# A two-block transformer kernel on one core: 80 steps of the experts' hidden layer in two-part float32r, and hi and lo runs of weights in pairs

## The chip, the cores and the metric

The kernel runs on one core of one Trainium2 chip. The metric is device time in microseconds, from the start of one execution to its end. TensorE (PE) multiplies, VectorE (DVE), ScalarE (ACT) and GpSimd (POOL) do the elementwise work, and SyncE (SP) issues most of the DMA transfers. Weights come from HBM once each; nothing is kept from one execution to the next.

## The reference

One input of 256 tokens by 2048 features goes through two blocks, all in float32. The first block is a mixer (a causal pooling half and a gated linear recurrence half), a projection `w_out`, and then a product-key expert layer. Its core, cut:

```python
def chunk(zc):                       # 128 tokens
    q = (zc @ peer_wq)...            # 8 heads, two halves of 128
    ... top 16 of each half, top 16 of their sums -> expert (16 of 16384 per head), gate = softmax
    u = jnp.take(peer_u, expert, axis=0)
    act = jax.nn.gelu(jnp.einsum('chkd,cd->chk', u, zc))
    v = jnp.take(peer_v, expert, axis=0)
    w = gate * act
    return jnp.einsum('chk,chkd->cd', w, v)
```

The second block projects to queries, keys, values, gates and a gated convolution (`w_in_2`), attends, merges (`w_sb_out_2`, `w_conv_out_2`, `w_o_2`), and ends in a feed-forward part: `relu(h @ w_up)**2 @ w_down`, 2048 to 8192 and back.

## The kernel before

Features lie on the 128 partitions, tokens along the free axis: a matmul takes 128x128 weights as its stationary operand and the tokens as its moving one. The program is a list of **steps**, filled in order and then played by one loop at the end of the kernel. A step is 128 output features; it has two halves, each with a **piece** of weights of 512 KB (`[128, 8, 128]` float32), so a half is 8 matmuls (k = 0 to 7).

There are two kinds of steps. A **plain** step (`whole_step`, matmuls on line 188) multiplies the weights `wx` as they came, in plain float32. An **f32r** step (`k16` and `k8x2`) splits weights and activations: ACT copies `wx` into `wh` (type float32r, line 1354, the hi part), DVE, in one stage with POOL, writes `wl = wx - wh` (line 1365, the lo part), and the activations are held as two parts side by side, `z[:, k, 0]` and `z[:, k, 1]`. A half is then a run of 8 **hi** matmuls (line 123, `wh` times both parts, 512 columns) and a run of 8 **lo** matmuls (line 126, `wl` times the first part, 256 columns). `k16` accumulates over 2048 features, two halves into one PSUM tile; `k8x2` over 1024, each half its own.

The expert layer avoids a gather of u and v rows for most tokens: for 176 of the 256 (`ND`), all 16384 experts' hidden values are computed, 128 steps of u (`u_step`: the plain product of `peer_u` with `zn`, the normalized tokens; `post_u` applies Gelu into one of seven `hidden` buffers of 8 steps each), then multiplied by a scattered gate matrix (`make_w`, line 863, with the list `Gt` that comes from a buffer `Gd` in HBM), and 128 v steps add the products with `peer_v` into the residual `R` (`post_v`, line 904). The first 48 u steps (`LEAD`) stand alone; then u and v steps alternate, u first, and the last 48 v steps stand alone again. For the other 80 tokens (`NG`), the rows are fetched: 160 **units**, each an indirect DMA of 1 MB by POOL (line 740) into one of three buffers `ga`, and a pass of DVE over 128x2048 elements (lines 756 and 764). Units are placed along the plain pieces at an even distance.

Weights come through a **ring** of 12 tiles of 512 KB (`stream`, `RING`). `take` hands out the next tile and asks that the one 12 before has been read in program order; `wx`, `wh` and `wl` of a piece each take one. `ahead(p)` issues the transfers of coming pieces on SP: always up to piece p + 3, and in a row of plain pieces as far as the ring goes. In the loop, piece p's matmuls follow `hi(p + 3)` on ACT and stand ahead of `lo(p + 3)` on DVE. `tick` lets the waiting tasks (evacuations, `make_w`) add their instructions after each piece, `need` ticks until a named result has been put into the program. `tasks` are ticked every time, `bg` ones while a budget lasts. Each engine works through its own instructions in program order.

PSUM has four accumulators (`mm`). The base pool holds R, the two-part activations (tag A), and two buffers B0 and B1 that hold, one after the other, the mixer's outputs, the search lists, hidden values, attention outputs and feed-forward activations.

## Time and profile before

| | |
|---|---|
| median of 3 runs | 2977.0 us (2976.8 to 2977.24) |
| the profiled execution | 2975.82 us |
| its span, first to last instruction | 2974.1 us |
| PE, DVE, ACT, POOL busy | 2941.1, 1916.8, 1079.7, 348.5 us |
| first and last plain u matmul; first and last v matmul (starts) | 348.8, 1382.8; 628.8, 1623.8 us |

The profile has the span in 40 slices of 74 us; in the rows of digits each is the busy share in tenths. In groups, `x` is the number of instructions, then come the busy time in us, the mean of one in ns, and the engine's idle time ahead of them with what ended it. Matmuls overlap, so the time that one costs is the distance between starts, not its own duration. One plain float32 matmul has two records on PE, one of f32r has one.

### The profile page before, as it was taken

What the parts mean: (1) busy time and instruction counts of PE and PEld (TensorE: products, weight loads), DVE (VectorE), ACT (ScalarE), POOL (GpSimd) and SP (SyncE); (2) the same over time, 40 slices, a digit from 0 to 9 for tenths busy, and PEclk for the clock granted to TensorE, in tenths of its full rate; (3) what the DMA queues carried; (4) which work ended last, traced back from release to release, by engine and by line L of the source; (5) the groups of instructions that cost most, each with busy time, mean ns of one, the idle gap of its engine ahead of it and who ended that gap; (6) DMA issues with size and microseconds to landing.
All of it is one profiled execution on the core that took longest, in us unless ns stands there. A gap on an engine that the chain in (4) does not pass through costs nothing.

```text
span 2974.1 us, 46400 instructions
## 1 busy us (share of the span) xinstructions
PE 2941.1 (99%) x18156; PEld 2735.0 (92%) x18156; DVE 1916.8 (64%) x3260; ACT 1079.7 (36%) x1774; POOL 348.5 (12%) x321
## 2 busy tenths in 40 slices
PE   9999999999999999999999999999999999999997
PEld 7888999999999999999999888888887888888886
DVE  8877885644444444445524889886658667776777
ACT  7755325500000000000003676657555444444444
POOL 0102221112122222222102000001500000000000
PEclk9999999999999999999999999999999999999999
DMA  6465699999999999999965555555654655555553
GB/s 235 159 200 197 212 306 344 352 387 414 395 396 395 392 400 399 398 393 395 388 219 169 176 172 179 183 174 192 204 181 145 203 191 188 186 172 198 198 191 128
DMA packets 208619, 773.46 MB, mean 260 GB/s; under 512 B 21536, under 2 KB 44384, under 8 KB 187488
## 3 DMA queue, kind: packets, MB, share of 16 engines
q1 hardware_dynamic: 161136, 588.46, 56.0%
q0 software_dynamic: 23984, 169.31, 14.4%
q10 hardware_dynamic: 23280, 12.72, 1.4%
q8 instruction: 144, 2.36, 0.3%
q14 instruction: 75, 0.61, 0.1%
HBM read 755.25 MB, written 13.63 MB: 259 GB/s over the span
## 4 chain that ended last, share of the span: by engine, by line
PE 94%; DVE 2%; ACT 2%; DMA 1%; issue 1%; SPq 0%; ACTq 0%; DVEq 0%
PE mm L188 41%; PE mm L123 33%; PE mm L126 17%; PE g L800 1%; DMA Gd<-gst 1%; DVE wl L1365 1%; ACT wh L1354 0%; DMA wx<-in_w_in_dram 0%; PE s L586 0%; PE g L778 0%; DMA R<-in_x_dram 0%; DVE R L1461 0%; PE s L246 0%; DVE Y L1460 0%; DMA wx<-in_w_down_dram 0%
## 5 line engine op out<-in xcount | busy, mean ns | idle before, releaser
L1354 ACT ACTIVATE wh<-wx 128x1024 fp32r<-128x1024 f32 (+1 forms) x579 | 609.2, 1054 | 682.2 <-PE mm L123 286.0
L1365 DVE TENSOR_TENSOR wl<-wx,wh 128x1024 fp32r<-128x1024 f32 (+2 forms) x579 | 694.9, 1207 | 158.7 <-ACT wh L1354 152.7
L123 PE MATMUL mm<-z,wh 128*128 128x512 f32 x2816 | 718.0, 397 | 12.9 <-ACT wh L1354 7.0
L188 PE MATMUL mm<-zn,wx 128*128 128x176 f32 x4096 | 633.3, 313 | 0.0
L188 PEld LDWEIGHTS mm<-zn,wx 128*128 128x128 f32 x4096 | 614.5, 190 | 0.1
L123 PEld LDWEIGHTS mm<-z,wh 128*128 128x128 f32 x2816 | 510.1, 190 | 109.5 <-ACT wh L1354 7.5
L904 DVE TENSOR_TENSOR R<-R,mm 128x176 f32<-128x176 f32 x256 | 86.1, 336 | 536.4 <-PE mm L188 532.1
L126 PEld LDWEIGHTS mm<-z,wl 128*128 128x128 f32 x2816 | 384.2, 191 | 29.6 <-DVE wl L1365 2.4
L126 PE MATMUL mm<-z,wl 128*128 128x256 f32 x2816 | 393.0, 283 | 1.1 <-DVE wl L1365 0.9
L188 PE MATMUL mm<-hd,wx 128*128 128x176 f32 x2048 | 313.5, 313 | 0.0
L188 PE MATMUL mm<-hb,wx 128*128 128x176 f32 x2048 | 312.7, 313 | 0.0
L188 PEld LDWEIGHTS mm<-hd,wx 128*128 128x128 f32 x2048 | 307.5, 190 | 0.0
L188 PEld LDWEIGHTS mm<-hb,wx 128*128 128x128 f32 x2048 | 306.9, 190 | 0.0
L123 PE MATMUL mm<-f,wh 128*128 128x512 f32 x1024 | 256.7, 392 | 0.2 <-DVE f L1261 0.2
L123 PEld LDWEIGHTS mm<-f,wh 128*128 128x128 f32 x1024 | 184.2, 189 | 33.5 <-DVE f L1261 0.7
L853 ACT ACTIVATE hd<-mm 128x176 f32<-128x176 f32 x64 | 20.3, 317 | 422.1 <-PE mm L188 412.8
L853 ACT ACTIVATE hb<-mm 128x176 f32<-128x176 f32 x64 | 20.3, 317 | 402.6 <-PE mm L188 393.4
L740 POOL DMA_INDIRECT ga<-in_peer_v_rows_dram,idx x80 | 107.0, 1338 | 399.0 <-DVE ga L764 214.8
L740 POOL DMA_INDIRECT ga<-in_peer_u_rows_dram,idx x80 | 99.7, 1246 | 449.3 <-DVE hid L756 378.8
L756 DVE CUSTOM_DVE_ANT_0 ga<-ga 128x2048 f32<-128x2048 f32 x64 | 146.0, 2284 | 7.3 <-DMA ga<-in_peer_u_rows_dram,idx 7.3
L126 PEld LDWEIGHTS mm<-f,wl 128*128 128x128 f32 x1024 | 139.7, 190 | 9.9
L764 DVE SCALAR_TENSOR_TENSOR ga<-ga,hid 128x2048 f32<-128x2048 f32 x63 | 147.8, 2346 | 0.2
(373 smaller groups left out, 2528.4 us busy)
## 6 DMA issues: line engine op xcount, KB each, us to landing
wx<-in_peer_u_dram SPq DMA_DIRECT2D x256, 512.0 KB
wx<-in_peer_v_dram SPq DMA_DIRECT2D x256, 512.0 KB
wx<-in_w_in_dram SPq DMA_DIRECT2D x191, 512.0 KB
wx<-in_w_up_dram SPq DMA_DIRECT2D x128, 512.0 KB
wx<-in_w_down_dram SPq DMA_DIRECT2D x128, 512.0 KB
wx<-in_w_out_dram SPq DMA_DIRECT2D x32, 512.0 KB
wx<-in_peer_wq_dram SPq DMA_DIRECT2D x32, 512.0 KB
wx<-in_w_o_dram SPq DMA_DIRECT2D x32, 512.0 KB
```

The costliest lines, as they stand in the source:

```text
L123: pe.matmul(ps, w[0][:, k], z[:, k0 + k], start=first and k == 0, stop=False, skip_group_check=True)
L126: pe.matmul(ps[:, 0], w[1][:, k], z[:, k0 + k, 0], start=False, stop=last and k == 7, skip_group_check=True)
L188: pe.matmul(ps, w[:, k], rhs(half, k), start=k == 0 and (split or half == 0), stop=k == 7 and (split or half == 1), skip_group_check=True)
L740: pool.indirect_dma_start(out=x, out_offset=None, in_=rows, in_offset=bass.IndirectOffsetOnAxis(ap=st["idx"][i][:, s:s + 1], axis=0))
L756: dve.tensor_tensor_reduce(out=x, in0=x, in1=y, scale=1.0, scalar=0.0, op0=ALU.mult, op1=ALU.add, accum_out=h[:, s:s + 1])
L764: dve.scalar_tensor_tensor(y, x, h[:, s:s + 1], y, op0=ALU.mult, op1=ALU.add)
L800: pe.matmul(p[:, t], A[:, t], B[:, t], start=True, stop=True)
L853: act.activation(hidden(g)[:, i], ps, AF.Gelu_apprx_tanh)
L904: dve.tensor_tensor(R[:, k, NG:], R[:, k, NG:], ps, op=ALU.add)
L1354: act.activation(w[:, i:i + n], x[:, i:i + n], AF.Copy)
L1365: dve.tensor_tensor(w[:, i:i + m], x[:, i:i + m], h[:, i:i + m], op=ALU.subtract)
```

## The change

1. **u steps 48 to 127 in parts** (`part_step`): hi weights times both parts of z (352 columns), lo weights times the last `LOW` = 176 of these columns, which are the part that `parts_of_z` writes at index 1, the rounded one. `z[:, k, 1]` is the copy in float32r and `z[:, k, 0]` what is left. `post_u_part` adds the two halves of the 352 columns (ACT copy, DVE addition) and applies Gelu. The first 48 u steps and all v steps stay plain. A u step now follows the v step three places later in the list: v steps 0 to 3 stand alone, then u and v alternate.
2. **k16 steps without lag** put both hi runs ahead of both lo runs (`own["rest"]`); their `wl` tiles count as read at the end of the second half. Steps with lag (the first two or three of a stage) and `k8x2` keep their order.
3. **The ring** may look ahead over pieces in parts, which count three tiles (`n` in `ahead`); `kind` tells "whole", "part" and None apart, and the budget of `tick` is 2.1, 0.7 and 1.25.
4. **Room**: B0 and B1 become one tile B; `zr` takes the place of `zn` once the plain u steps are done with it; the second set of fetched tokens gets its transposed rows (`zt1`) only once G is built; some small tiles move to other pools.

The core of the diff:

```diff
-    def product(ps, w, z, k0, first, last):
+    def product(ps, w, z, k0, first):
         for k in range(8):
             pe.matmul(ps, w[0][:, k], z[:, k0 + k], start=first and k == 0, stop=False, skip_group_check=True)
             yield
+
+    def rest(ps, w, z, k0, last):
         for k in range(8):
             pe.matmul(ps[:, 0], w[1][:, k], z[:, k0 + k, 0], start=False, stop=last and k == 7, skip_group_check=True)
             yield
...
-            yield from product(own["ps"], w, zt, k0, half == 0, half == 1)
+            yield from product(own["ps"], w, zt, k0, half == 0)
+            if lag:
+                yield from rest(own["ps"], w, zt, k0, half == 1)
+            elif half == 0:
+                own["rest"] = rest(own["ps"], w, zt, k0, False)
+            else:
+                yield from own.pop("rest")
+                yield from rest(own["ps"], w, zt, k0, True)
...
+    def part_step(src, post, needs=((), ())):
+        own = {}
+        def lows(half, w):
+            for k in range(8):
+                z = st["zr"][:, 8 * half + k].rearrange("p a t -> p (a t)")
+                pe.matmul(own["ps"][:, 2 * ND - LOW:], w[1][:, k], z[:, 2 * ND - LOW:], start=False,
+                          stop=half == 1 and k == 7, skip_group_check=True)
+                yield
+        def mm(half, w):
+            if half == 0:
+                own["ps"] = accumulator().rearrange("p a t -> p (a t)")[:, :2 * ND]
+            for k in range(8):
+                pe.matmul(own["ps"], w[0][:, k], st["zr"][:, 8 * half + k].rearrange("p a t -> p (a t)"),
+                          start=half == 0 and k == 0, stop=False, skip_group_check=True)
+                yield
+            if half == 0:
+                own["rest"] = lows(0, w)
+            else:
+                yield from own.pop("rest")
+                yield from lows(1, w)
+                tasks.append(post(half, own["ps"]))
...
+    def parts_of_z():
+        r = rs["rs2"]
+        z = st["zr"] = st["pb"].tile([128, 16, 2, ND], F32R, name="zr", tag="zn")
+        last = None
+        for k in range(17):
+            if k < 16:
+                t = tmp.tile([128, T], F32, name="zk", tag="ev", bufs=5)[:, :ND]
+                dve.scalar_tensor_tensor(t, R[:, k, NG:], v("norm2_g", k), r[:, NG:], op0=ALU.mult, op1=ALU.mult)
+                act.activation(z[:, k, 1], t, AF.Copy)
+            if k > 0:
+                dve.tensor_tensor(z[:, k - 1, 0], last, z[:, k - 1, 1], op=ALU.subtract)
+            last = t
+            if k % 4 == 0:
+                yield
+        ready.add("zr")
...
+            h = hidden(g)[:, i]
+            yield
+            act.activation(h, ps[:, :ND], AF.Copy)
+            yield
+            dve.tensor_tensor(h, h, ps[:, ND:], op=ALU.add)
+            release("mm")
+            yield
+            act.activation(h, h, AF.Gelu_apprx_tanh)
...
+                if j == 0 and g == 0:
+                    begin.append(lambda: tasks.append(parts_of_z()))
...
-                if e < 128:
-                    u_step(e)
                 whole_step([a["peer_v"][16 * g + 2 * j], a["peer_v"][16 * g + 2 * j + 1]],
...
+                if 48 <= e - 3 < 128:
+                    part_step(src("peer_u", e - 3), post_u_part(e - 3), (["zr"], ()))
...
-            if q > p + 3 and (q > p + RING - 2 or not all(plain(i) for i in range(p, q + 1)) or not ring[-RING][1]):
+
+            n = 1 + 2 * sum(not plain(i) for i in range(p + 3, q + 1))
+            if q > p + 3 and (n > RING - 2 or not (kind(p) and kind(q)) or not all(r[1] for r in ring[-RING:][:n])):
                 return
...
-                read(q, "wx", "wh", "wl")
-        tick(2.1 if plain(p) else 1.25)
-        if "units" in st and plain(p):
+                read(q, "wh", *(["wx"] if plain(q) else []))
+
+                if not long:
+                    read(q, "wl")
+                elif half:
+                    read(q - 1, "wl")
+                    read(q, "wl")
+        tick({"whole": 2.1, "part": 0.7, None: 1.25}[kind(p)])
+        if "units" in st and kind(p):
```

PE in the first block's `w_in`, two steps, before: `mm` is the accumulator, `z1` the activations.

```order
L123 MATMUL mm_415<-z1_99,wh_322 128x512 x8
L126 MATMUL mm_415<-z1_99,wl_343 128x256 x8
L123 MATMUL mm_415<-z1_99,wh_347 128x512 x8
L126 MATMUL mm_415<-z1_99,wl_371 128x256 x8
L123 MATMUL mm_487<-z1_99,wh_376 128x512 x8
L126 MATMUL mm_487<-z1_99,wl_409 128x256 x8
```

The same place in the changed program (its lines 125 and 131):

```order
L125 MATMUL mm_414<-z1_99,wh_321 128x512 x8
L125 MATMUL mm_414<-z1_99,wh_346 128x512 x8
L131 MATMUL mm_414<-z1_99,wl_342 128x256 x8
L131 MATMUL mm_414<-z1_99,wl_362 128x256 x8
L125 MATMUL mm_486<-z1_99,wh_367 128x512 x8
L125 MATMUL mm_486<-z1_99,wh_412 128x512 x8
```

The lo run of the first half has moved behind the hi run of the second; the matmuls are the same.

PE where u and v steps alternate, before (`zn` marks u, `hb` and `hd` the hidden values of a v step):

```order
L188 MATMUL mm_6276<-zn_2527,wx_6142 128x176 x8
L188 MATMUL mm_6276<-zn_2527,wx_6157 128x176 x8
L188 MATMUL mm_6300<-hd1_3998,wx_6170 128x176 x8
L188 MATMUL mm_6312<-hd1_3998,wx_6183 128x176 x8
L188 MATMUL mm_6326<-zn_2527,wx_6196 128x176 x8
L188 MATMUL mm_6326<-zn_2527,wx_6209 128x176 x8
L188 MATMUL mm_6348<-hd1_3998,wx_6224 128x176 x8
```

And in the changed program, a pair and the first rows of the next:

```order
L201 MATMUL mm_7967<-hb_4302,wx_7861 128x176 x8
L201 MATMUL mm_7985<-hb_4302,wx_7891 128x176 x8
L225 MATMUL mm_8000<-zr_5605,wh_7935 128x352 x8
L225 MATMUL mm_8000<-zr_5605,wh_7965 128x352 x8
L217 MATMUL mm_8000<-zr_5605,wl_7961 128x176 x8
L217 MATMUL mm_8000<-zr_5605,wl_7979 128x176 x8
L201 MATMUL mm_8047<-hb_4302,wx_7981 128x176 x8
L201 MATMUL mm_8061<-hb_4302,wx_7983 128x176 x8
```

A u step's two pieces of plain weights have become four runs from four converted tiles, while v keeps its two.

DVE at the first v step, before: `hd<-hd,Gt` are the eight multiplications of the first hidden group, `ga` a fetched unit, `R<-R,mm` the first v results.

```order
L756 ISA ga,hid_3933<-ga 128x2048
L756 ISA hid_3933 128x1
L863 TENSOR_TENSOR hd_3622<-hd_3622,Gt 128x176 x2
L756 ISA ga,hid_3933<-ga 128x2048
L756 ISA hid_3933 128x1
L863 TENSOR_TENSOR hd_3622<-hd_3622,Gt 128x176 x3
L756 ISA ga,hid_3933<-ga 128x2048
L756 ISA hid_3933 128x1
L863 TENSOR_TENSOR hd_3622<-hd_3622,Gt 128x176 x3
L756 ISA ga,hid_3933<-ga 128x2048
L756 ISA hid_3933 128x1
L904 TENSOR_TENSOR R<-R,mm 128x176 x2
```

The same place in the changed program, up to the first pair of `parts_of_z` (lines 632 and 635):

```order
L944 TENSOR_TENSOR hd_3624<-hd_3624,Gt 128x176 x2
L822 ISA ga,hid_3917<-ga 128x2048
L822 ISA hid_3917 128x1
L944 TENSOR_TENSOR hd_3624<-hd_3624,Gt 128x176 x3
L632 SCALAR_TENSOR_TENSOR zk<-R,vec,ra_2604 128x176
L944 TENSOR_TENSOR hd_3624<-hd_3624,Gt 128x176
L632 SCALAR_TENSOR_TENSOR zk<-R,vec,ra_2604 128x176
L635 TENSOR_TENSOR zr<-zk,zr 128x176
```

Three more such pairs follow, then the seventh multiplication, four pairs, the eighth, and seven pairs less one; only then come two more rows of a unit and the first additions into R. The work on `zr` has come between the multiplications that the first v matmuls read.

## Rows read from the trace of the kernel before

**Rows 1.** The page: busy time, and the 40 slices' PE clock and DMA rate.

```profile
PE 2941.1 (99%) x18156; PEld 2735.0 (92%) x18156; DVE 1916.8 (64%) x3260; ACT 1079.7 (36%) x1774; POOL 348.5 (12%) x321
...
PEclk9999999999999999999999999999999999999999
...
GB/s 235 159 200 197 212 306 344 352 387 414 395 396 395 392 400 399 398 393 395 388 219 169 176 172 179 183 174 192 204 181 145 203 191 188 186 172 198 198 191 128
```

**Rows 2.** The page's groups: line, engine, operation, count, busy us, mean ns, idle before.

```profile
L1354 ACT ACTIVATE wh<-wx 128x1024 fp32r<-128x1024 f32 (+1 forms) x579 | 609.2, 1054 | 682.2 <-PE mm L123 286.0
L1365 DVE TENSOR_TENSOR wl<-wx,wh 128x1024 fp32r<-128x1024 f32 (+2 forms) x579 | 694.9, 1207 | 158.7 <-ACT wh L1354 152.7
L123 PE MATMUL mm<-z,wh 128*128 128x512 f32 x2816 | 718.0, 397 | 12.9 <-ACT wh L1354 7.0
L188 PE MATMUL mm<-zn,wx 128*128 128x176 f32 x4096 | 633.3, 313 | 0.0
...
L904 DVE TENSOR_TENSOR R<-R,mm 128x176 f32<-128x176 f32 x256 | 86.1, 336 | 536.4 <-PE mm L188 532.1
...
L188 PE MATMUL mm<-hd,wx 128*128 128x176 f32 x2048 | 313.5, 313 | 0.0
L188 PE MATMUL mm<-hb,wx 128*128 128x176 f32 x2048 | 312.7, 313 | 0.0
...
L853 ACT ACTIVATE hd<-mm 128x176 f32<-128x176 f32 x64 | 20.3, 317 | 422.1 <-PE mm L188 412.8
```

**Rows 3.** Timeline of PE at the first v step: start us, us, instructions, count.

```profile
628.76 4.94 PE L188 MATMUL mm<-hd,wx 128*128 128x176 f32 x32
633.53 4.94 PE L188 MATMUL mm<-zn,wx 128*128 128x176 f32 x32
```

**Rows 4.** Timeline of PE in the down projection.

```profile
2704.88 2.00 PE L123 MATMUL mm<-f,wh 128*128 128x512 f32 x8
2706.72 1.12 PE L126 MATMUL mm<-f,wl 128*128 128x256 f32 x8
2707.67 2.00 PE L123 MATMUL mm<-f,wh 128*128 128x512 f32 x8
```

**Rows 5.** Timelines of weight loads at 16 columns and of PE at 128.

```profile
1512.87 1.01 PEld L778 LDWEIGHTS g<-sel,zt 128*128 128x128 f32 x8
1513.80 4.78 PEld L188 LDWEIGHTS mm<-hb,wx 128*128 128x128 f32 x32
...
575.90 1.05 PE L800 MATMUL g<-hb,hb 128*128 128x128 f32 x8
576.79 2.55 PE L188 MATMUL mm<-zn,wx 128*128 128x176 f32 x16
```

**Rows 6.** The alternating stretch: busy us (count) by engine, PE clock, DMA share, GB/s.

```profile
628.80:1387.50 758.70, 758.70 (x5088) 758.70 (x5088) 348.62 (x417) 25.73 (x82) 162.79 (x120) 1.00 1.00 398
```

**Rows 7.** Waits of SP's queue, 700 to 1400 us: total, times, longest.

```profile
SPq L1330 <- PE mm L188: 569.5, 291, 2.0
```

**Rows 8.** DMA queues, 640 to 700 us: packets, MB, share.

```profile
q1 hardware_dynamic: 4031, 14.71, 61.3%
q0 software_dynamic: 1374, 10.07, 40.5%
```

**Rows 9.** Timelines of PE in a woven hi run, two windows that end at 2252.2.

```profile
2250.00 2.43 PE L123 MATMUL mm<-z,wh 128*128 128x512 f32 x10
...
2250.90 1.52 PE L123 MATMUL mm<-z,wh 128*128 128x512 f32 x6
```

**Rows 10.** Timeline of DVE ahead of the first v step; zn's durations.

```profile
619.15 0.86 DVE L863 TENSOR_TENSOR hd<-hd,Gt 128x176 f32<-128x176 f32 x2 [18.41 <-DMA Gt<-Gd]
619.93 2.28 DVE L756 CUSTOM_DVE_ANT_0 ga<-ga 128x2048 f32<-128x2048 f32 x1
...
625.52 1.25 DVE L863 TENSOR_TENSOR hd<-hd,Gt 128x176 f32<-128x176 f32 x3
...
L573 DVE SCALAR_TENSOR_TENSOR zn<-R,vec,ra x16: 387/391/1156, 261.2 to 284.0; 128x176 f32<-128x176 f32 x16
```

More of the change, by code (lines that the diff above doesn't have):

```diff
@@ L27 @@
 ND = T - NG
+LOW = ND
 EPS = 1e-6
@@ L192, in mm @@
                 tasks.append(post(half, ps))
-        steps.append((src, mm, needs, begin, 0, False, True))
+        steps.append((src, mm, needs, begin, 0, False, "whole", False))
+    def part_step(src, post, needs=((), ())):
[19 more added lines that the diff above has]
+                tasks.append(post(half, own["ps"]))
+        steps.append((src, mm, needs, None, 0, False, "part", True))
     R = base.tile([128, 16, T], F32, name="R")
@@ L698, in token_rows @@
         ga = st["ga"] = base.tile([128, 4, 2048], F32, name="ga", tag="A")
-        st["zt"] = [ga[:, 3] if i == 0 else pb.tile([128, 2048], F32, name=f"zt{i}") for i in range(len(SETS))]
+        st["zt"] = [ga[:, 3]]
         for i, (t0, n) in enumerate(SETS):
+            if i == 1:
+                yield from wait("G")
+            zg = st["zg"] if i == 0 else st["zg1"]
             for q in range(4):
@@ L842, in hidden @@
             return st[key]
[L843 removed]
+        return st["hb"][i - 3]
     def load_G(g):
@@ L1306, with kind @@
     NP = len(pieces)
+    def kind(p):
+        return steps[pieces[p][0]][6]
     def plain(p):
-        return steps[pieces[p][0]][6]
+        return kind(p) == "whole"
     ring = []
@@ L1413 @@
         s, half = pieces[p]
-        _, mm, needs, begin, lag, weave, _ = steps[s]
+        _, mm, needs, begin, lag, weave, _, long = steps[s]
         ahead(p)
```

66 lines of the change are left out of this document (39 added, 27 removed).

## The prediction

> **What bounds the kernel now.** I read the page's busy line and its slices first. TensorE is busy 2941.1 us of 2974.1, at full clock in all 40 slices: the chip is bound by the matmuls, and a change counts by what it takes off PE's queue or by the waits that it puts there [rows 1]. The slices also show the second limit: in slices 9 to 20 the DMA engines move 387 to 414 GB/s, twice what they move in the second half. Then the groups: the plain float32 steps (L188) hold 633 + 314 + 313 = 1260 us of PE, and the f32r hi and lo runs (L123, L126) most of the rest, without idle time worth naming in front of them [rows 2]. The timeline of the stage in which u and v steps alternate shows one step of each, 32 records long: 628.76 to 633.53, 4.77 us a step and 9.55 us a pair, or 149 ns a record of 176 columns; a matmul of plain float32 is two such records, 298 ns [rows 3]. The timeline of the down projection gives the price of f32r: a run of eight hi matmuls of 512 columns takes 1.84 us (2704.88 to 2706.72), 230 ns each, eight lo matmuls of 256 columns 0.95 us, 119 ns each [rows 4].
>
> **Edit 1: the u steps 48 to 127 in parts.** Each loses 16 matmuls of 298 ns (4.77 us) and gets 16 hi matmuls of 352 columns and 16 lo matmuls of 176. Neither width is in the trace.
> - Hi, 352 columns: from below, the plain record, which streams twice 176 columns in 149 ns [rows 3]; from above, the 512-column matmul of 230 ns less its 160 columns more, which at 2.4 GHz are 67 ns: 163 ns [rows 4]. The cost of the same kind of operand is the nearer one; I take 160.
> - Lo, 176 columns: from above, the 256-column matmul, 119 ns [rows 4]; from below, the same in proportion, 119 x 176/256 = 82 ns. Between them stands the weight load. In the additions of the fetched rows the moving operand has 16 columns, and still eight weight loads take 0.93 us (1512.87 to 1513.80), 116 ns each; the one-hot products of 128 columns go at 0.89/8 = 111 ns [rows 5]. So small columns do not go below some 110 ns when every matmul has new weights, and each lo matmul has. I take 114. The Trainium skill, "TensorE: Matmul & The Clock Gate", section "LDWEIGHTS (loading the stationary operand)", says that a load costs its columns over 1.2 GHz, 107 ns for 128 columns: the narrower lo operand would then buy only the step from 119 to 107, the rows above agree within 10 ns, and by it the step below would be 4.27 us instead of 4.38.
>
> The step is then 16 x (160 + 114) = 4.38 us, 0.39 us less than 4.77, and 80 steps give 31 us. With 163 and 119 it is 4.51 us, 21 us in all; with 149 and 82 it is 3.70 us, 86 us in all, as far as PE goes.
>
> What comes with it lies beside PE. ACT: 160 conversions of 1.054 us, and per step a copy and a Gelu of 0.32 instead of one Gelu: 169 + 25 us on an engine that is busy 25.7 of the 758.7 us of that stage. DVE: 160 subtractions of 1.207 us and 80 additions of 0.34: 193 + 27 us on top of 348.6 [rows 2, 6]. That makes 569 us in some 730, 78%; the lo weights of a step stand in DVE's queue three pieces ahead of the piece that uses them, behind at most a gather unit of 2.3 us [rows 10] and the additions into R. The cover is there, though no longer thick.
>
> **Edit 2: the ring.** A u piece now takes three of the 12 slots (wx, wh, wl), so a pair takes 8 instead of 4. Before, a v or u piece is asked for when the piece eleven before it is done, 11 x 2.39 = 26.2 us ahead; SP spends 569.5 us of the 700 us looked at waiting for PE to free a slot, so the ring is always full [rows 7]. In the changed program the buffer for the first half of a v step is freed by the first hi run of the u step one pair earlier: what is left of that step (1.28 + 1.82), a v step (4.77) and a u step (4.38), 12.2 us. Requests come in bursts of up to five pieces, 2.6 MB; with the gathers beside them the weights' queue moved 14.71 MB in the 60 us of its busiest stretch, 245 GB/s [rows 8], so the last of five lands 10.7 us after the first is asked for. That fits, without much to spare. Cost taken: nothing by itself; but see the next term.
>
> **The stage's other floor.** Weights, gathers and G lists of the pair stage are 398 GB/s over 758.7 us = 302 MB, 3.80 MB a pair, with the engines' share at 1.00 [rows 6]. None of these bytes go away, and the gathers are spread over pieces, not over time. In its busiest stretch, 640 to 700 us, the two large queues moved 14.71 + 10.07 MB in 60 us, 413 GB/s [rows 8]. At that rate a pair cannot take less than 9.20 us; PE wants 4.77 + 4.38 = 9.15. The gain of edit 1 is therefore capped at 0.35 us a pair, 28 us, and since two queues at their limit do not interlock without a loss I take one more off and book 27.
> The Trainium skill, "DMA: Bandwidth & Descriptors", section "Where 436 GB/s comes from", puts the limit of HBM transfers at about 358 GB/s per core and the fabric's at 435. The trace stands above the first already, so only the second can be a ceiling here; by it a pair could go down to 8.74 us and PE alone would decide.
>
> **Edit 3: both hi runs, then both lo runs.** It applies to the 193 of 208 steps over 2048 that have no lag. Bytes and matmuls are the same; there are half as many changes from lo to hi. The only longer hi runs of before are those woven in front of w_up. Two windows with the same end show ten matmuls from 2250.00 and six from 2250.90: four starts in 0.90 us, 225 ns each, against the mean of 230 of a run of eight [rows 4, 9]. So a hi run begins slow and settles at some 226. If the second eight go at 226, a step gains 8 x 4 = 32 ns, 6 us over 193 steps. What a lo run of 16 costs against two of eight no row here tells; I allow it 8 ns a step and book 4.5 us. Bounds: 0 and 9. DVE and ACT see the same distances from a freed slot to its use as before, because what is read later is also needed later; nothing new waits.
>
> **Edit 4: zr.** The z parts are built in zn's place when the last plain u step has read it, and DVE's order puts that work into the multiplication of the first hidden group by its G list. Before, G's list lands at 619.15 and the eight multiplications are done by 626.8 (625.52 + 1.25), 2 us ahead of the first v step at 628.76 [rows 3, 10]. Now the first v step is due one u step earlier, at 624.0, and the last two multiplications stand behind nine and seventeen instructions of zr, the second half of a pair waiting for ACT and for the last plain u matmul. At 0.39 us each for those with R and 0.34 for a subtraction [rows 2, 10], after 619.15: two multiplications, a gather unit and three more end at 623.3; the sixth at 624.1; the seventh at 627.5 (a zk, the wait for PE and ACT, then four subtractions with three zk); the eighth 3.3 us later, at 630.8. PE does six matmuls by 625.8 and ends the run at 631.1 instead of 626.4: 4.7 us once, say 5, bounds 2 and 9. The first parts are wanted at 648; zr is done by some 637.
>
> **Sum.** Against the profiled execution, 2975.8 us (span 2974.1 and 1.7 around it): -27 (edit 1 under the DMA floor) -4.5 (edit 3) +5 (edit 4) = -26.5, 2949.3. The median of the runs is 1.2 us above that execution: **2950 us**.
>
> **Rivals.**
> - *The lo run follows its columns* (82 ns). PE's pair would be 4.77 + 3.87 = 8.64, and the DMA floor of 9.20 decides: -28 -4.5 +5, 2949. Only if the DMA engines also go well beyond 413 GB/s does it show: 72 us at the most, 2905. Against it: the 16-column rows. The part below 2934: chance 0.08.
> - *f32r keeps its overhead*: 163 and 119, and 4 us of DMA losses: a gain of 21 - 4 - 5 = 12 us without edit 3, 2965. A row for each half of it exists. Chance 0.16 for 2960 to 2971.
> - *The DMA engines are already full*: a share of 1.00 over the whole stage would say so. Then a pair stays at 9.55, PE waits for weights by 0.39 us a pair, and only edits 3 and 4 are left: 2977. For it the share, against it that PE, DVE and SP wait for one another and hardly for a transfer, and the 413 GB/s of the busiest stretch. Chance 0.08.
> - *The ring starves PE* (slower): with 12.2 us instead of 26.2, a v piece that stands behind a gather in the DMA queues comes late. It decides from 0.39 us a pair on; at 1 us a pair the stage loses 80 x 0.6 = 48 us: 3026. For it, 10.7 of 12.2 us are already used by a burst; against it, the first piece of a burst needs only 2.1 us. Chance 0.1.
>
> **Numbers.** The forecast (2934 to 2960) holds 0.58. Faster than before by over 0.2% (6 us, about what a measurement of this kernel can tell from no change): 0.58 + 0.08 + 0.16 = 0.82. Within 0.2%: 0.08. Slower: 0.10. The range leaves out the starved ring and the fastest case, 0.18 together, and reaches to the case in which the DMA engines are already full: 2934 to 2978.
>
> **What would show it.** In the changed trace a u step of 16 hi and 16 lo matmuls lasts 4.3 to 4.5 us; lo matmuls start 110 to 119 ns apart; pairs follow each other at 9.15 to 9.3 us; the DMA engines move 408 to 416 GB/s there; PE waits some 5 us for DVE in the first v run; a step over 2048 takes 5.56 instead of 5.58 us. I am wrong if PE waits for wh (that is, for weights behind it) throughout the stage, if the lo matmuls start 85 ns apart, or if DVE's lo weights come late behind the gather units.

## The result and the profile after

The changed kernel takes 2991.8 us (median of 7 runs, 2985.8 to 2999.7), the kernel before 2977.2 us beside it (7 runs, 2975.0 to 2979.9): a ratio of 1.0052, interval 1.0042 to 1.0062. It is **slower by 0.5%**, where 2950 us and a gain of 0.9% were forecast. The profiled execution took 2999.73 us (span 2998.0). That is 8 us above the median and the longest of the seven, so its waits stand at the upper end of what this kernel shows.

The page of the changed kernel, the lines that answer to [rows 1]: busy time with share and count, and the DMA rate in 40 slices.

```profile
PE 2929.1 (98%) x18156; PEld 2718.3 (91%) x18156; DVE 2118.7 (71%) x3532; ACT 1265.6 (42%) x2031; POOL 358.1 (12%) x321
...
GB/s 235 156 183 196 232 312 338 357 345 382 400 383 385 385 376 394 396 400 400 413 228 172 182 174 171 175 193 186 187 195 139 195 179 188 184 196 185 195 197 134
```

In these profiled executions PE is busy 12 us less than before and the program is 24 us longer: what PE saved, and more, went into waits. In slices 10 to 18, in the alternating stage, the DMA rate was 392 to 414 GB/s and is 376 to 400. The groups that answer to [rows 2] name the wait: the last column is the idle time in front of the group, and what ended most of it.

```profile
L1443 ACT ACTIVATE wh<-wx 128x1024 fp32r<-128x1024 f32 (+1 forms) x739 | 778.5, 1055 | 1102.3 <-DMA wx<-in_peer_u_dram 364.9
...
L225 PE MATMUL mm<-zr,wh 128*128 128x352 f32 x1280 | 237.1, 336 | 22.9 <-ACT wh L1443 22.7
```

PE waits in the hi runs for ACT, and ACT for the weights of peer_u. The timeline of PE in that stage shows one pair without a wait and one with it (start, us, line, count; in brackets the idle time ahead and what ended it); it answers to [rows 3].

```profile
999.57 4.97 PE L201 MATMUL mm<-hb,wx 128*128 128x176 f32 x32
1004.25 2.87 PE L225 MATMUL mm<-zr,wh 128*128 128x352 f32 x16
1006.96 1.92 PE L217 MATMUL mm<-zr,wl 128*128 128x176 f32 x16
1008.71 4.97 PE L201 MATMUL mm<-hb,wx 128*128 128x176 f32 x32
1013.49 1.56 PE L225 MATMUL mm<-zr,wh 128*128 128x352 f32 x8
1017.29 1.54 PE L225 MATMUL mm<-zr,wh 128*128 128x352 f32 x8 [2.25 <-ACT wh L1443]
```

The first pair takes 9.14 us (999.57 to 1008.71), where 9.15 was forecast. In the second the eight hi matmuls of the second half come 2.25 us late. Over the stage this happens often enough to count: the row of all zr hi matmuls gives their first and last start, and from that, less the 15 hi matmuls of the last step (2.4 us), a pair takes (1414.6 - 648.4 - 2.4) / 79 = 9.67 us, against 9.55 before.

```profile
L225 PE MATMUL mm<-zr,wh x1280: 317/324/661, 648.4 to 1414.6; 128*128 128x352 f32 x183
```

Tables of waits (who waited for whom: us in total, times, longest) follow the wait back. PE in 640 to 1420 us:

```profile
PE mm L225 <- ACT wh L1443: 22.7, 19, 2.2
PE mm L201 <- DMA wx<-in_peer_v_dram: 1.7, 2, 1.5
```

ACT in 700 to 1400 us:

```profile
ACT wh L1443 <- DMA wx<-in_peer_u_dram: 332.5, 116, 10.2
```

And SP's queue in 700 to 1400 us, which answers to [rows 7]:

```profile
SPq L1417 <- DVE wl L1454: 218.7, 87, 8.0
SPq L1417 <- DMA wx<-in_peer_u_dram: 178.3, 68, 8.3
SPq L1417 <- PE mm L225: 88.8, 62, 5.4
```

Before, SP waited for PE alone, 569.5 us of the 700: PE set the pace and the weights stood ready. Now SP, which asks for the weights, waits mostly for a subtraction and for transfers of peer_u. (Rows of the same table that name the additions `hd` and `hb`, 54.6 and 25.5 us, belong to the subtractions too: these requests start within 0.06 us of the end of one.) That is a closed circle: a request waits for a slot, the slot for a subtraction (wl), the subtraction for the conversion (wh), the conversion for a transfer that was itself asked for too late. The chain of waits that ends in the hi run at 939.99 shows one turn of it.

```profile
927.40 1.14 DVE wl L1454
...
928.56 10.22 DMA wx<-in_peer_u_dram
...
938.89 1.06 ACT wh L1443
...
939.99 2.14 PE mm L225 x8
```

The slot came free at 928.5, with a subtraction whose weights PE used in the lo run that began at 928.07; by the program's order it stands three pieces ahead of its use. It came so late because its conversion ended only at 925.96 and DVE was in a pass over a fetched unit until 927.4. The transfer took 10.22 us, the conversion 1.06, and PE stood 2.2 us. The table of transfers gives the landing times over the whole run (KB each, median us from issue to landing) and, for comparison, those of the first stage. The last line is the alternating stage alone, 640 to 1380 us, both tables together: the median there is 8.6 us, the longest 15.4.

```profile
wx<-in_peer_u_dram SPq DMA_DIRECT2D x256, 512.0 KB, 7.1
wx<-in_peer_v_dram SPq DMA_DIRECT2D x256, 512.0 KB, 9.0
wx<-in_w_in_dram SPq DMA_DIRECT2D x191, 512.0 KB, 3.7
...
DMA to landing us min/median/max: 3.4/8.6/15.4
```

Such a wait can cost more than its length. The window behind that one (busy us of PE, PEld, DVE, ACT, POOL, then PE clock, DMA share, GB/s) shows a granted clock of 0.66, that is, partly at 1.2 instead of 2.4 GHz. PE had waited 1.46 us at 931.45 and 2.20 at 939.99. The DMA rate is 274 GB/s there: SP had issued no request between 930.1 and 937.5, and the queue ran low. Not every wait does it: behind the 2.25 us at 1017.29, shown above, the clock stayed at 1.00.

```profile
940.00:945.00 5.00, 5.00 (x26) 5.00 (x27) 4.26 (x7) 1.56 (x3) 0.82 (x1) 0.66 0.70 274
1017.00:1022.00 5.00, 4.71 (x35) 4.71 (x36) 4.73 (x6) 1.86 (x4) 0.47 (x1) 1.00 0.90 314
```

The eight hi matmuls from 939.99 take 1.94 us up to the next run at 941.93, where sixteen took 2.71 in the pair without a wait. The Trainium skill, "TensorE: Matmul & The Clock Gate", section "HAM oscillation — how this bites in real kernels", describes this: waits for transfers between groups of matmuls let the clock fall, and the next group starts slow. The trace agrees at 940 us, where the clock was 0.66, and not at 1017.

### The profile page after: what moved, and what is told of

Read it like the earlier page. It is cut to its first block, busy times and chain, and to the rows that moved or that the text cites. A ratio compares the mean times of both kernels' runs of the same rounds, so it can differ in the third digit from the quotient of the medians.

```text
span 2998.0 us, 47069 instructions
## 1 busy us (share of the span) xinstructions
PE 2929.1 (98%) x18156; PEld 2718.3 (91%) x18156; DVE 2118.7 (71%) x3532; ACT 1265.6 (42%) x2031; POOL 358.1 (12%) x321
## 4 chain that ended last, share of the span: by engine, by line
PE 57%; DMA 8%; DVE 2%; ACT 1%; issue 0%; SPq 0%; ACTq 0%; DVEq 0%
PE mm L125 28%; PE mm L131 14%; PE mm L201 10%; DMA wx<-in_peer_u_dram 6%; PE mm L225 2%; PE mm L217 2%; DMA wx<-in_peer_v_dram 1%; DMA Gt<-Gd 1%; ACT wh L1443 1%; DVE wl L1454 1%; DMA wx<-in_w_up_dram 0%; PE g L844 0%; DVE R L1556 0%; DVE ga L830 0%; DVE Y L1555 0%
## 5 line engine op out<-in xcount | busy, mean ns | idle before, releaser
L1443 ACT ACTIVATE wh<-wx 128x1024 fp32r<-128x1024 f32 (+1 forms) x739 | 778.5, 1055 | 1102.3 <-DMA wx<-in_peer_u_dram 364.9
L1454 DVE TENSOR_TENSOR wl<-wx,wh 128x1024 fp32r<-128x1024 f32 (+2 forms) x739 | 890.7, 1213 | 486.2 <-ACT wh L1443 455.5
L125 PE MATMUL mm<-z,wh 128*128 128x512 f32 x2816 | 691.3, 396 | 13.2 <-ACT wh L1443 6.8
L131 PE MATMUL mm<-z,wl 128*128 128x256 f32 x2816 | 367.1, 283 | 1.0 <-DVE wl L1454 1.0
L225 PE MATMUL mm<-zr,wh 128*128 128x352 f32 x1280 | 237.1, 336 | 22.9 <-ACT wh L1443 22.7
L201 PE MATMUL mm<-zn,wx 128*128 128x176 f32 x1536 | 238.6, 313 | 0.0
L225 PEld LDWEIGHTS mm<-zr,wh 128*128 128x128 f32 x1280 | 210.4, 192 | 29.5 <-ACT wh L1443 29.2
L201 PEld LDWEIGHTS mm<-zn,wx 128*128 128x128 f32 x1536 | 229.5, 191 | 0.1
L217 PE MATMUL mm<-zr,wl 128*128 128x176 f32 x1280 | 157.8, 277 | 0.4 <-DVE wl L1454 0.4
L217 PEld LDWEIGHTS mm<-zr,wl 128*128 128x128 f32 x1280 | 157.1, 196 | 1.0 <-DVE wl L1454 0.8
```

The costliest lines, as they stand in the source:

```text
L125: pe.matmul(ps, w[0][:, k], z[:, k0 + k], start=first and k == 0, stop=False, skip_group_check=True)
L131: pe.matmul(ps[:, 0], w[1][:, k], z[:, k0 + k, 0], start=False, stop=last and k == 7, skip_group_check=True)
L201: pe.matmul(ps, w[:, k], rhs(half, k), start=k == 0 and (split or half == 0), stop=k == 7 and (split or half == 1), skip_group_check=True)
L217: pe.matmul(own["ps"][:, 2 * ND - LOW:], w[1][:, k], z[:, 2 * ND - LOW:], start=False, stop=half == 1 and k == 7, skip_group_check=True)
L225: pe.matmul(own["ps"], w[0][:, k], st["zr"][:, 8 * half + k].rearrange("p a t -> p (a t)"), start=half == 0 and k == 0, stop=False, skip_g ...
L1443: act.activation(w[:, i:i + n], x[:, i:i + n], AF.Copy)
```

## The experiments

Every run is compared with the kernel before on the same chip, 2976.0 to 2976.5 us (median of 8 to 15 runs).

**What the parts of the change are worth.** First the u steps go back to plain float32, with all else of the change kept:

```
-  part_step(src("peer_u", e - 3), post_u_part(e - 3), (["zr"], ()))
+  u_step(e - 3)
-  if j == 0 and g == 0:
-      begin.append(lambda: tasks.append(parts_of_z()))
```

> Edit 1 undone alone: the 80 u steps of the changed program are plain float32 again, no z parts are built, the ring hands out slots one a piece as before; the order of v and u steps, both hi then both lo runs, and all else of the change stay. Theory 'late weights' (the loss sits in the alternating stage, because a u step in parts takes six of the 12 slots and a v piece is then asked for only three pieces, some 7 us, ahead, while it takes 9.0 us to land): the loss of the changed kernel is gone; 2970 to 2974 us if both hi then both lo runs are worth the 4.5 us of the prediction, 2976 to 2981 if they are worth nothing, as the stages behind the last v step say (1332.4 us before, 1336.6 after). Rival 'the new order of the runs does the harm': still at 2985 or more.

2978.6 us (2974.2 to 2984.2, 11 runs), 1.0011 of before, 1.0002 to 1.0020. The loss is gone, so it sits in the u steps in parts. But the new order of the runs gains nothing that this time shows. The reverse, the old order with the u steps in parts:

```
-  elif half == 0:
-      own["rest"] = rest(own["ps"], w, zt, k0, False)
-  else:
-      yield from own.pop("rest")
-      yield from rest(own["ps"], w, zt, k0, True)
+  yield from rest(own["ps"], w, zt, k0, half == 1)
```

> Edit 3 undone alone: a step over 2048 takes hi, lo, hi, lo again, the u steps stay in parts. Theory 'late weights': nothing changes in the alternating stage, so 2985 to 2996 us, within 5 us of the changed kernel; if the new order of the runs is what costs the 4.2 us behind the last v step, the steps there take that much less. Rival 'the new order does the harm': back to 2975 or less.

2993.4 us (1.0061, 1.0048 to 1.0075): as slow as the change, with the same wait of PE in 640 to 1420 us.

```profile
PE mm L219 <- ACT wh L1437: 22.6, 20, 2.1
```

**Is it the lead of the requests?** The same 12 slots, but a new buffer takes the slot that has been free the longest, not the next in turn (the edit, cut):

```
-  return stream.tile([128, 8, 128], dtype, name=what, tag="w")
+  return stream.tile([128, 8, 128], dtype, name=what, tag=f"w{i}", bufs=1)
...
+  def free():
+      return [i for i in range(RING) if last[i] is None or last[i][1]]
+  def slot():
+      return min(free(), key=lambda i: freed[i], default=None)
...
+  n = 1 + (kind(p + 3) == "part")
-  if q > p + 3 and (n > RING - 2 or not (kind(p) and kind(q)) or not all(r[1] for r in ring[-RING:][:n])):
+  if q > p + 3 and (not (kind(p) and kind(q)) or len(free()) < n):
```

> The changed kernel with the same 12 slots, but a new buffer takes the slot that has been free the longest instead of the next one in a fixed turn. Bytes, matmuls and conversions are the same; only how long ahead a weight piece can be asked for changes: by the program's order 9 to 10 pieces before its use for all pieces, where the fixed turn gives a v piece 4 in every second pair and 5 to 8 else. Theory 'late weights': PE's waits for wh in 700 to 1400 us fall from 22.7 us to under 5, a pair takes 9.2 to 9.35 us, the whole 2955 to 2970 us. Rival 'the DMA engines are full' (3.8 MB a pair at 387 to 400 GB/s are 9.5 to 9.8 us whenever they are asked for): pairs stay at 9.6 to 9.75 us and the whole at 2983 to 2996 us. Rival 'ACT and DVE are late': no change either, with DVE's subtractions ending later than the pieces that use them.

**2950.0 us** (0.9913, 0.9899 to 0.9927), 42 us below the change and 26 below the kernel before. In 640 to 1420 us PE waits for nothing. The row of its zr hi matmuls:

```profile
L225 PE MATMUL mm<-zr,wh x1280: 320/323/443, 648.9 to 1373.5; 128*128 128x352 f32 x183
```

The timeline of PE in the same place as above:

```profile
1000.70 4.97 PE L201 MATMUL mm<-hb,wx 128*128 128x176 f32 x32
1005.38 2.86 PE L225 MATMUL mm<-zr,wh 128*128 128x352 f32 x16
1008.08 1.92 PE L217 MATMUL mm<-zr,wl 128*128 128x176 f32 x16
1009.84 4.97 PE L201 MATMUL mm<-hb,wx 128*128 128x176 f32 x32
```

SP's waits in 700 to 1400 us, the longest and those behind subtractions:

```profile
SPq L1428 <- PE mm L217: 243.6, 147, 3.0
SPq L1428 <- DVE hd L932: 122.3, 34, 4.7
SPq L1428 <- DVE hb L932: 108.9, 30, 4.5
...
SPq L1428 <- DVE wl L1465: 39.6, 10, 5.0
```

And two windows, with the columns of the windows above, the changed kernel first and then the any-slot run:

```profile
700.00:1000.00 300.00, 288.52 (x1979) 285.29 (x1978) 212.24 (x281) 83.27 (x126) 56.39 (x47) 0.99 0.98 386
...
700.00:1000.00 300.00, 300.00 (x2102) 300.00 (x2101) 226.54 (x293) 86.76 (x133) 66.21 (x49) 1.00 1.02 413
```

A pair takes (1373.5 - 648.9 - 2.4) / 79 = 9.14 us, PE's own price. SP now waits 283 us for PE, against 111. What has gone from its table are the waits for transfers: 31 us (20.7 for peer_v, 10.6 for peer_u) where the changed kernel has 178 for peer_u. Waits for subtractions are still there, 271 us against 299: the rows of `hd` and `hb` belong to them, since these requests too start within 0.06 us of the end of a subtraction. With a long lead they cost PE nothing. The DMA engines move 413 GB/s where in the changed kernel they moved 386 (700 to 1000 us), and ACT and DVE do the same work as there: neither was the limit. Transfers land even later (median 11.5 us in 640 to 1380, against 8.6), but they are asked for 9 to 10 pieces ahead, some 20 us.

Whether the DMA rate bounds the stage at all was asked with gathers cut to a quarter. This kernel leaves most of the rows of the fetched tokens out, so that their part of the output is not computed; DVE's instructions of the same kind and size work on other factors (the edit, cut):

```
-  pool.indirect_dma_start(out=x, out_offset=None, in_=rows,
-                          in_offset=bass.IndirectOffsetOnAxis(ap=st["idx"][i][:, s:s + 1], axis=0))
+  m = 32 if u % NG >= 3 else 128
+  pool.indirect_dma_start(out=x[:m], out_offset=None, in_=rows,
+                          in_offset=bass.IndirectOffsetOnAxis(ap=st["idx"][i][:m, s:s + 1], axis=0))
```

> The changed kernel with its gathers cut: all but the first three units of each table fetch 32 of the 128 rows, 0.25 MB instead of 1 MB, and work on stale rows for the rest (the fetched tokens' part of the output is left out by that; the products with v's rows take the gates as factors instead of the hidden values, in instructions of the same kind and size). DVE's, ACT's and PE's work is the same, the DMA engines lose some three quarters of 126 MB in the alternating stage. Theories 'late weights' and 'DMA engines full' both expect that PE's waits for wh go: pairs at 9.1 to 9.2 us, 2948 to 2958 us, which is PE's own price of the change; the landing of a v piece should fall from 9.0 to under 6 us. Rival 'ACT and DVE are late, 78% busy': the waits stay, 2975 us or more.

2950.4 us (0.9915, 0.9900 to 0.9930), at 286 to 303 GB/s from 700 us on; the median landing is 6.8 us in 640 to 1380, and PE waits 0.6 us. A pair takes (1375.0 - 649.3 - 2.4) / 79 = 9.16 us. Short leads with quick landings, or late landings with long leads, both give 2950: the loss needs a short lead and late landings together. DVE and ACT are as busy here as in the changed kernel, so their load alone is not the cause.

**The lead by itself.** The kernel before, with plain float32 throughout, and with only the slots of the alternating stage reduced, here to 4, in the second run to 6 (`slot()` then looks at the first `few[0]` slots):

```
+  few[0] = 4 if 2 * st["P0"] <= q < 2 * st["P0"] + 320 else RING
```

> The kernel before, with plain float32 in all u steps, and nothing changed but the slots that the pieces of the alternating stage may use: 4 of the 12, so that each piece is asked for when the piece four before it has been read, three pieces or 7.2 us of PE's time ahead, against eleven pieces or 26 us. No conversion stands in this circle: PE itself frees every slot. Theory 'late weights': with no change of the work the lead alone makes PE wait; in the changed kernel a v piece landed 9.0 us after its request and a u piece 7.1 us, so 0 to 1 us are lost a piece where landing is longer than 7.2 us, 320 pieces, 2990 to 3150 us; PE's waits in 640 to 1390 us are for transfers. If a request that stands in the queue with two others instead of ten lands in 5 us or less, the time stays at 2976 and the lead of 7 us was long enough: then the late conversions, not the short turn of the slots, are what makes the changed kernel wait. Rival 'the DMA engines are full': 2976 us, since the bytes are the same.

> The same with 6 slots: five pieces, 12 us ahead, the lead that the prediction ascribed to the changed kernel. Theory 'late weights': a lead of 12 us covers the landing times of 7 to 9 us, 2976 to 2984 us; and by as much less than with 4 slots as the queue is deeper. Rival 'the DMA engines are full': 2976 us.

4 slots: 3077.7 us (1.0348, 1.0332 to 1.0364). 6 slots: 2980.4 us (1.0014, 1.0005 to 1.0024). PE's waits in 640 to 1390 us with 4 slots:

```profile
PE mm L188 <- DMA wx<-in_peer_u_dram: 39.6, 36, 2.5
PE mm L188 <- DMA wx<-in_peer_v_dram: 15.6, 15, 5.4
```

And with 6:

```profile
PE mm L188 <- DMA wx<-in_peer_u_dram: 2.9, 2, 2.4
```

No work has changed, and there is no subtraction in the circle; 7.2 us of lead cost 102 us, 12 us cost 4, 26 us nothing. With 4 slots the median landing in 640 to 1380 us was 6.4 us, below the lead, and the longest 13.8: it is the late ones of the 320 pieces that PE waits for, in 51 waits. That a late request delays the one behind it is likely but not shown.

```profile
DMA to landing us min/median/max: 3.5/6.4/13.8
```

And the any-slot rule with fewer slots, 9 here and 10 in the second run:

```
+  few[0] = 9 if p < NP - 3 and kind(p + 3) and 2 * st["P0"] - 40 <= p < 2 * st["P0"] + 300 else RING
```

> The any-slot run with only 9 of the 12 slots in the alternating stage: by the program's order each weight piece is asked for 6 to 7 pieces before its use, evenly, where the changed kernel has 4 to 8 (6.4 on average) and the any-slot run 9 to 10. Work, conversions and rule are those of the any-slot run. Theory 'late weights' (the lead decides, by whatever rule it comes): most of the loss is back, 2970 to 2995 us, with PE waiting for wh and for transfers in 700 to 1400. Rival 'the fixed turn itself costs, for instance because a slot that one late subtraction holds stops all requests behind it': an even lead of 6 to 7 pieces is enough, 2950 to 2956 us.

> The same with 10 slots: each piece is asked for 7 to 8 pieces before its use. Theory 'late weights': between the runs with 9 and with 12 slots, 2952 to 2970 us. Rival 'the fixed turn itself costs': 2950 to 2953 us, as with 12 slots.

9 slots: 3001.3 us (1.0080, 1.0063 to 1.0097), even above the 2995 expected. 10 slots: 2963.4 us (0.9963, 0.9949 to 0.9977). PE's waits in 640 to 1420 us with 9:

```profile
PE mm L225 <- ACT wh L1456: 29.5, 26, 4.0
```

And with 10:

```profile
PE mm L225 <- ACT wh L1456: 7.2, 7, 1.4
```

With 6 to 7 pieces the any-slot rule is no better than the fixed turn: the rule as such does nothing, and a shorter lead under the same rule costs. But the count of pieces does not give the price by itself. The fixed turn goes down to 4 pieces and loses 42 us against the any-slot run, the 9 slots never go below 6 and lose 51, and 6 pieces cost 4 us in the kernel before, where PE frees every slot. With 9 slots SP waits 223.8 us for transfers of peer_u in 700 to 1400 us, with 12 it waits 10.6: there too a request waits for the landing and conversion of an earlier piece. No run takes the conversions alone out of that circle, and the kernel before also moves fewer bytes in the same time (398 against 413 GB/s), so why 6 pieces are worth so little here stays open. The control, the rule in the kernel before:

> The control: the kernel before with the any-slot rule for its 12 slots and nothing else. There PE waits for no weight in the alternating stage and takes one slot a piece, so the fixed turn costs nothing. Theory 'late weights': no difference, 2974 to 2978 us. Rival 'the rule itself makes a kernel faster, elsewhere than in the alternating stage': 2970 or less, and the any-slot run owes that part of its gain to it.

2974.7 us (0.9994, 0.9985 to 1.0003): no difference.

**The order of the runs where nothing waits.** The any-slot kernel with the old order of hi and lo, by the edit shown above:

> The kernel of the any-slot run with hi, lo, hi, lo in the steps over 2048: what both hi then both lo runs are worth where PE waits for nothing in the alternating stage. From the distances of matmuls in the runs so far (hi 228.6 against 230.1 ns, lo 119.5 against 119.1, 16 each a step) the new order is worth 18 ns a step, 3.4 us over 193 steps: this run 3 to 4 us above the any-slot run, 2953 to 2954 us. If the new order adds waits of its own for DVE or ACT, as 2.6 us for f in the run with plain u steps hint: 2950 or less.

2951.2 us against 2950.0 (0.9918 against 0.9913, both with an interval of 0.0014 to either side, 4 us). The times neither show nor exclude the 3.4 us that the distances of matmuls give. The traces say more. The stretch from the last v matmul to the end of the span takes 1347.2 us in the any-slot run (1601.4 to 2948.5) and 1347.1 to 1347.3 in the four other runs with that rule and the new order, and 1350.2 to 1351.4 in all six traces with the old order. With the fixed turn and the new order it takes 1350.7, 1351.7 and, in the change, 1354.5. So with the any-slot rule the new order gains 3 to 4 us in that stretch, and with the fixed turn no gain is to be seen there. In the whole time this is hidden, as the first u matmul starts anywhere from 345.5 to 350.0 us in these traces.

**Edit 4.** In the any-slot kernel the first v steps take 24.46 us where their 128 records are 19.07. Two other places for zr's parts; the last two lines are in the second run only:

```
-  if j == 0 and g == 0:
+  if j == 1 and g == 0:
       begin.append(lambda: tasks.append(parts_of_z()))
...
-  if k % 4 == 0:
+  if k == 8:
       yield
```

> The kernel of the any-slot run, and zr's z parts put into DVE's queue one v step later, behind the eight multiplications of the first hidden group. There the first four v steps took 24.46 us where 128 records of 149 ns are 19.07: 5.4 us of PE. Theory (edit 4 as the prediction has it: DVE's order makes the first v run wait): the two waits for hd of 1.31 and 2.08 us go, the first hi run of zr starts some 5 us earlier, the whole is 5 us less than the any-slot run, 2945 us. Rival: the multiplications come late anyway, since G's list lands at 619; then the waits stay and the time too. Rival: zr itself is now late for its first u step, and the 5 us come back there.

2957.4 us, 7.4 more than without it. The waits for hd are gone and worse ones have come: the multiplications for the second group now stand ahead of zr's last parts, and DVE waits for their G list. The timeline of DVE:

```profile
643.37 0.47 DVE L944 TENSOR_TENSOR hd<-hd,Gt 128x176 f32<-128x176 f32 x1 [7.08 <-DMA Gt<-Gd]
```

And of PE at the first u step in parts, whose second half then waits 1.71 us more:

```profile
646.88 2.69 PE L225 MATMUL mm<-zr,wh 128*128 128x352 f32 x8 [4.19 <-DVE R L985]
```

> The kernel of the any-slot run, with zr's parts queued on DVE behind the eight multiplications of the first hidden group, as in the run before, but in two pieces of time instead of five, so that all of zr stands ahead of the multiplications of the second group. In the run before, five zr parts stood behind those, and DVE waited 7.1 us (to 643.4) for the second G list before it could make them; PE then waited 4.2 + 1.7 us in the first u step. Theory (the 5.4 us of edit 4 are only DVE's order): PE's waits for hd go and none come at the first hi run of zr, 5 us less than the any-slot run, 2945 us. Rival: the additions into R, now queued behind 6 us of zr, hold PE's accumulators, and the first four v steps still take 22 us or more: 2950.

2951.4 us: no gain either. The rival was right in substance: zr's 12 us of DVE work now hold back the additions into R, these hold PE's accumulators, and the first v steps still take 23.74 us (622.53 to 646.27) by the timeline of PE.

```profile
622.53 14.48 PE L201 MATMUL mm<-hd,wx 128*128 128x176 f32 x96
639.83 6.72 PE L201 MATMUL mm<-hd,wx 128*128 128x176 f32 x32 [2.82 <-DVE R L985]
646.27 2.87 PE L225 MATMUL mm<-zr,wh 128*128 128x352 f32 x16
```

## Why the prediction was wrong, step by step

**The step that failed is edit 2**, the ring: a lead of 12.2 us and "Cost taken: nothing by itself". In its place the runs showed 22.7 us of waits of PE for wh and a pair of 9.67 us instead of some 9.2; with the same work and a longer lead both are gone. Three things in the step were wrong.
- *The lead.* I followed one slot and took it for all. A pair takes eight slots of twelve, so the turn shifts from pair to pair. Counted through in the program's order (at which piece the last reader of each slot stands; SP asks in order), a piece of v's first half is asked for 4 pieces ahead in one pair and 7 in the next, second halves 5 and 8, u's pieces 6 to 8. Four pieces ahead leaves three pieces of PE's time: a v half 2.39, u's first hi run 1.28, its second and both lo runs 3.07, together 6.7 us. PE's waits are not where this count is shortest, though: 1.7 us are for pieces of v, and 22.7 us for wh, that is, for pieces of u with a counted lead of 6 to 8. Six pieces ahead leaves 10 to 11.5 us of PE's time, out of which a u piece needs its landing, 8.6 us in the median and 15.4 at the longest, and 1.06 us of conversion.
- *Who frees the slot.* I reckoned with PE's pace. But the slot of a u piece's raw weights is freed by DVE, whose subtraction is planned three pieces ahead, but comes just in time as soon as one transfer is late. Then the free slot is late too, and the next request. The chain at 939.99 shows one such turn, and SP's table the waits for transfers (178.3 us for peer_u, 10.6 in the any-slot run). Its waits for subtractions are no proof, as the any-slot run has 271 us of them without a loss. How much of the price is this circle, and how much the short lead, no run separates.
- *The landing.* I used the rate of the busiest stretch for a burst, 10.7 us for the fifth piece and 2.1 us for the first. Landing is not that even: 9.0 us is the median of all v pieces, and in the alternating stage the longest took 15.4. The Trainium skill, "DMA: Bandwidth & Descriptors", section "Anatomy of one DMA — SWDGE (gpsimd) path", has a fit of some 2 us and the bytes at 436 GB/s, for transfers issued by GpSimd: 3.2 us for 512 KB, an estimate. The trace has 3.7 us where little else moves (these transfers are issued by SP), and two to three times that beside the gathers.

My rival "the ring starves PE", chance 0.1, is what happened, with its place and direction, and with half the price that I gave it: 9.67 against PE's 9.14 is 0.53 us a pair, 42 us in 79 pairs. That is the profiled execution, the longest of the seven and 49 us above that of the any-slot run; that the medians of the two kernels differ by 42 us too is in part chance. "PE waits for wh" was also the first sign of being wrong that I had named. In the starts of PE's matmuls from 640 to 1420 us, 29.8 of these are in 27 gaps and about 10 in slower matmuls, at the lower clock (0.53 to 0.66 in four windows of 4 to 11 us, one of them shown above). The leads could have been counted from the order, and against a burst of 10.7 us the 6.7 us would have made 0.1 far too low; the price does not follow from the count.

**Edit 1, PE's price: right.** A pair takes 9.14 us against 9.15. Its u step starts 4.46 us before the next step (1005.38 to 1009.84), 4.38 was forecast, and its v step takes 4.68 instead of 4.77; the 0.09 us only change sides. The last v record is followed after 28 ns, the first hi matmul after 282, together as much as 149 and 161, and at the change from hi to lo nothing is lost. Within the runs hi matmuls are 161 ns apart in the mean and lo ones 110 to 113, against 160 and 114. The lo run did not follow its columns. Where the weights are in time, 80 x (9.55 - 9.14) = 33 us come back.

**The DMA floor: not a floor at 9.20.** With 413 GB/s, the very rate of [rows 8], the any-slot run makes pairs of 9.14 us, and with a quarter of the gathered rows still 9.16. PE decides, and 27 instead of 31 us was too careful. The rate itself was not passed, so whether more than 413 GB/s can be had is not shown. The stage was limited by when the weights were asked for, not by the rate.

**Edit 3: the distances are right, the times do not show it.** The second eight hi matmuls do go at 226 to 227 ns, 228.6 in the mean against 230.1, and lo at 119.5 against 119.1; that is 16 x 1.5 - 16 x 0.4 = 18 ns a step, 3.4 us. Undoing it cost 1.2 us in the any-slot kernel and 2.7 us by the ratios (1.0061 against 1.0052) in the changed one, each less than its interval, and with plain u steps the time is 2.6 us above before. "Nothing new waits" was too bold for so small a gain: in the profiled executions of the change and of the run with plain u steps PE waits 2.6 us for f, against 0.2 before; in the any-slot run, of the same order, it does not, and there the stretch behind the last v matmul is 3 to 4 us shorter than with the old order.

**Edit 4: right in its size, by two parts of which one was not in it.** Forecast was +5, the seventh multiplication done at 627.5, the eighth at 630.8, and some 5 us of PE waiting for DVE in the first v run. The PE timeline of the change has it, in the rows that answer to [rows 10]:

```profile
623.83 1.95 PE L201 MATMUL mm<-hd,wx 128*128 128x176 f32 x12
627.09 0.56 PE L201 MATMUL mm<-hd,wx 128*128 128x176 f32 x2 [1.31 <-DVE hd L944]
629.74 18.95 PE L201 MATMUL mm<-hd,wx 128*128 128x176 f32 x114 [2.08 <-DVE hd L944]
```

From 623.83 to the first hi run at 648.40 are 24.57 us for 19.07 us of work: 5.5 us. PE's waits for hd are 1.31 and 2.08 us, 3.4 instead of some 5, and the eighth multiplication is done at 629.7 instead of 630.8. Another 1.6 us are eleven records of 293 instead of 149 ns: the granted clock was 0.50 from 631 to 633 us, which no term of mine had. Moving zr elsewhere did not give them back.

**The sum** with the any-slot rule: 2975.8 - 33 + 5.5 = 2948.3, where 2950.0 was measured. Two more terms nearly cancel: the 3 to 4 us of edit 3, and some 4 us that the change costs once at 1420 us and that the prediction lacks. There DVE waits for a list of G, the additions into R stand behind it, and PE waits for one of them; the granted clock is 0.71 in the 5 us from 1420.

```profile
1419.59 0.86 DVE L944 TENSOR_TENSOR hb<-hb,Gt 128x176 f32<-128x176 f32 x2 [10.05 <-DMA Gt<-Gd]
...
1420.75 29.54 PE L201 MATMUL mm<-hb,wx 128*128 128x176 f32 x185 [2.16 <-DVE R L985]
```

The change has the same wait with 3.24 us at 1462.89; the kernel before and the run with plain u steps have none. That the sum meets the forecast of 2950 is no merit of the prediction, which was made for a kernel whose weights came late. The any-slot kernel beats both kernels.

## What to carry to other kernels

An edit that gives a step more buffers in a shared ring shortens the leads of the requests in it: count, for each position in the turn, which instruction frees the slot and how much of the bound engine's time lies between that and the use, and hold it against landing times of a loaded queue, tails included, and the conversions behind them. The count warns, but it is not a price: 6 pieces cost 4 us where PE freed every slot, and 6 to 7 cost 51 us where conversions stood between. Be wary of slots that are freed by an engine which itself waits for the transfer: one late piece can then make the next one late (read from one chain of waits, not isolated by a run). Where the lead is short and the space is used up, handing out the slot that has been free the longest, in place of the next in turn, can lengthen it (here 4 to 8 pieces became 9 to 10); in the kernel before, where nothing was short, the rule cost nothing.

## What the runs showed of the hardware

- How steep the price of a short lead is: with the same bytes and matmuls, 12, 10 and 9 slots gave 2950, 2963 and 3001 us, and in the kernel before 12, 6 and 4 slots 2976, 2980 and 3078 us. In both rows the last step costs several times the one before.
- The landing time of 512 KB grows with what stands in the queue and with what else is moved: in 640 to 1380 us the median was 6.4 us with 4 slots, 8.6 in the changed kernel, 11.5 in the any-slot run, which is the fastest, and 6.8 with a quarter of the gathered rows. A long landing alone says nothing of lateness.
- The DMA engines' share does not tell how full they are: it is 0.98 at 386 GB/s with PE waiting and 1.02 at 413 GB/s without. The prediction's rival of the full engines rested on such a 1.00 [rows 6].
- A wait of 2.2 us of PE, some 8.5 us behind one of 1.5 us, was followed by a granted clock of 0.66 over 5 us; behind one of 2.25 us it stayed at 1.00. Over the stage the changed kernel's profiled execution paid its gaps some 1.4 times (42 us lost for 30 us of gaps).
- Records of start can shift work between neighbours: 28 ns behind the last plain matmul and 282 behind the first f32r one are together the usual 149 and 161.
